# Zero rows under the second chunk product of a delta-rule layer, and a smaller scratch for dynamic DMAs

## The chip, the cores and the metric

The kernel runs on one core of one Trainium2 chip. The core has a matrix engine (TensorE, PE in the profile; its weight loads have a row of their own, PEld), and VectorE (DVE), ScalarE (ACT), GpSimd (POOL) and SyncE (SP), each with its own queue of instructions. The metric is device time in microseconds (us) of one execution, the median of several.

## The reference, cut to what matters

A trunk of two layers on 256 tokens of width 2048. Each layer has a mixing block (one projection whose columns feed RWKV-7 time mixing, dilated attention and a gated MLP, then one output projection) and a feed-forward block. All is float32. The change lies in the time mixing, whose core is the delta rule, 12 heads of 64 channels, one token after the other:

```
def step(state, inp):
    r_t, w_t, k_t, v_t, kk_t, a_t = inp
    sk = jnp.einsum('bhvk,bhk->bhv', state, kk_t)
    state = (state * w_t[:, :, None, :]
             - sk[..., None] * (kk_t * a_t)[:, :, None, :]
             + v_t[..., None] * k_t[:, :, None, :])
    return state, jnp.einsum('bhvk,bhk->bhv', state, r_t)
```

The kernel computes it in two chunks of 128 tokens: within a chunk, all tokens' inner products of two sequences of 64-vectors are formed by matrix products, a triangular matrix is inverted, and the state passes from the first chunk to the second once.

## The kernel before, in words

**The main stream.** Nearly all of TensorE's work is dense products with weights that come from memory in chunks of 512 KB. SP loads a chunk (`raw`), ACT rounds it to the fast format (`whi`, line 104), DVE forms the rest (`wlo`, line 113), and TensorE does three products for each piece of weights: high by high, high by low, low by high (lines 521 to 523 with 256 columns, lines 548 to 550 with up to 512).

**The order.** Python generators emit side work between the pieces of the stream. Each call of `slot()` advances every live generator by one `yield`; it is called about every 12 products of the stream. The order on every engine is thus fixed at build time.

**A pair.** `pair(j)` (line 731) handles heads 2j and 2j+1, one in rows 0 to 63, the other in rows 64 to 127; there are 6 pairs in each layer, 12 in all. For each pair the chunk matrices come from `products(ps)` (line 811), called twice: first for `be` (line 836, tiles `ps_1`), then for `ka` (line 859, tiles `ps_3`). A call goes over 2 heads and 2 chunks. For each it does one product over 128 rows (line 814: high and low parts of a head stacked in the stationary operand `Sp`, the high part of the moving operand twice in `Mv`) and one over the 64 rows of that head (line 815: the same `Sp`, the low part of the moving operand in `Lo`), both into one accumulator. All three lie in one tile, `spl`. A call is 8 products of 256 columns.

**Around a call.** After the first call ACT overwrites the high parts in `Sp` with those of `ka` (line 805), which has to wait until the products that read them are done, and DVE the low parts (line 809). DVE then masks the first results into `A` (line 840), ACT rounds them (`Ah`, line 843), DVE forms `M` (line 848) and `Tm` (line 849), and masks the second halves into `Aqb` (line 851), which frees the accumulators. The second call follows, and right behind it, in the same slot, TensorE transposes `Tm` (line 866, `ps_x`), into an accumulator that line 851 frees. Twelve products of the stream later comes the inversion's first level (line 896).

**The start of a layer.** `start()` (line 627) opens the layer's tiles and lets POOL clear some of them (line 661). In layer 0 POOL then computes the norm of the tokens (line 226) and issues the load of the masks `lvl` (line 398), which DVE waits for (line 184).

Of the kernel before, what the change touches and what calls it, by code (L numbers as in the profile page):

```python
# [20 lines left out]
P = 128  # L21
D = 2048
# [33 lines left out]
def tile_trunk(ctx, tc, x_d, xt_d, pos_d, cst_d, lvl_d, pcol_d, pcv_d, prow_d,  # L56
# [93 lines left out]
    def step(srcs, fn):  # L150
        """weight chunks and the emitter that consumes them"""
        chunks.extend(srcs)
        steps.append(fn)

# [23 lines left out]
    def setup(lvl8):  # L178
        """masks and rotary tables"""
        nc.gpsimd.dma_start(pos_i, pos_d)  # L180
        nc.gpsimd.dma_start(pcols[1], pcol_d[1])
        V.tensor_copy(ident_h, ident)
        yield
        V.tensor_copy(msk, lvl8[:, 6 * P:])
        yield
        V.tensor_copy(lvl.rearrange("p a b -> p (a b)"), lvl8[:, :6 * P])
        ready["tables"] = True
        yield
        pos_f = const.tile([P, 2], F32, name="pos_f")
        V.tensor_copy(pos_f, pos_i)  # L190
        ang = const.tile([P, 16], F32, name="ang")
        for i in range(2):
            V.tensor_scalar(ang[:, i * 8:(i + 1) * 8], cst[:, CS["inv"]:CS["inv"] + 8],
                            pos_f[:, i:i + 1], None, op0=ALU.mult)
        yield
        kr = const.tile([P, 16], F32, name="kr")
        magic = 12582912.0
        for period in (2 * math.pi * 4096, 2 * math.pi):
            V.tensor_scalar(kr, ang, 1.0 / period, magic, op0=ALU.mult, op1=ALU.add)
            V.tensor_scalar(kr, kr, magic, None, op0=ALU.subtract)  # L200
            yield
            rest = period
            for bits in (7, 7, 9, 0):
                if bits:
                    q = 2.0 ** (math.floor(math.log2(rest)) + 1 - bits)
                    c = math.floor(rest / q) * q
                else:
                    c = rest
                rest -= c
                V.scalar_tensor_tensor(ang, kr, -c, ang, op0=ALU.mult, op1=ALU.add)  # L210
            yield
        V.tensor_scalar(ang, ang, math.pi, -math.pi, op0=ALU.min, op1=ALU.max)
        yield
        A.activation(sin, ang, AF.Sin)
        A.activation(cos, ang, AF.Sin, scale=0.5)
        yield
        V.tensor_tensor(cos, cos, cos, op=ALU.mult)
        V.tensor_scalar(cos, cos, -2.0, 1.0, op0=ALU.mult, op1=ALU.add)

# [1 line left out]
    def rsqrt(out, ssq, scale, eps):  # L221
        """out = (ssq*scale + eps)^-0.5"""
        n = ssq.shape[-1]
        t = sm.tile([P, 24], F32, name="rs_t")
        V.tensor_scalar(t[:, :n], ssq, scale, eps, op0=ALU.mult, op1=ALU.add)
        G.tensor_tensor(out, t[:, :n], mhalf[:, :n], op=ALU.pow)

    def sumsq(src, acc, n, junk=None):
        """acc = sum of squares over the n (at most 512) columns of src"""
        if junk is None:  # L230
            junk = pmx.tile([P, 512], F32, name="junk", tag="mx")[:, :n]
        A.activation(junk, src, AF.Square, accum_out=acc)

    def t_block(src, gain):
        """src(i) -> [tok, 128] blocks; returns the split [128 ch, 256 tok] tile times gain"""
        ps = pmx.tile([P, S], F32, name="ps_t", tag="mx")
        for i in range(2):
            T.transpose(ps[:, i * P:(i + 1) * P], src(i), ident)
        ah = const.tile([P, S], F32R, name="act_hi", bufs=KT)
        al = const.tile([P, S], F32R, name="act_lo", bufs=KT)  # L240
        if gain is None:
            A.copy(ah, ps)
            V.tensor_tensor(al, ps, f(ah), op=ALU.subtract)
        else:
            A.activation(ah, ps, AF.Copy, scale=gain)  # L245
            V.scalar_tensor_tensor(al, ps, gain, f(ah), op0=ALU.mult, op1=ALU.subtract)  # L246
        return ah, al
# [7 lines left out]
    def take(n):  # L255
        """count n banks whose readers come later; they must be emitted before the banks go round"""
        while ready["banks"] + n > 4:
            slot()
        ready["banks"] += n
# [14 lines left out]
    def keep_warm(n):  # L274
        """products of zeros while the tensor engine has to wait: its clock falls when it idles"""
        ps = pmx.tile([P, 256], F32, name="ps_w0", tag="mx")
        for _ in range(2 * n):
            T.matmul(ps, warm[:, :P], warm, start=True, stop=True)

    def refresh(yg, yl, rs, c, i, on_dve=True, out=False):  # L280
        """x += yg * rs for one block of 512 columns of a token tile"""
# [10 lines left out]
    class Wave:  # L292
        """the first two column tiles of a product, k tile by k tile"""
# [6 lines left out]
        def part(self, kts, high):  # L300
            """the products with the high or the low parts of these k tiles"""
# [21 lines left out]
    def rows_of(ss, wait=4):  # L323
        """the reciprocal root mean square of the tokens, by partition and as a row on all of them"""
# [24 lines left out]
    def opening(gain0, act, tiles):  # L349
        """the first products, from x as it lies in DRAM by columns"""  # L350
# [59 lines left out]
    def boundary(l, gain0, act, post, tiles):  # L410
        """residual update by columns, the transposed and split input of the next product, and its first two
        column tiles as far as the k tiles have come; the statistics of x come behind"""
# [11 lines left out]
        def tr(g, i):  # L424
            """transposes of k tiles 2g, 2g+1 for one token tile"""
            if i == 0:
                banks[g] = pmm.tile([P, 2, S], F32, name="ps_t", tag="mm")
            for q in range(2):
                kt = 2 * g + q
                T.transpose(banks[g][:, q, i * P:(i + 1) * P], x[:, i, kt * P:(kt + 1) * P], ident)  # L430
# [79 lines left out]
    # products: weights stationary, [128 ch, 256 tok]  # L510
    def ws_step(src, act, out, after):
        """two chunks of 8 k tiles"""
# [20 lines left out]
    # products: activations stationary, 2 x [128 tok, n]  # L533
    def as_steps(src, off, act, k0, nk, n, after, tail=0, more=False, late=0, hold=False):
        """one step per chunk of two k tiles; the last ``tail`` chunks go token tile by token tile"""
# [71 lines left out]
    def mixing(l, post_in):  # L607
# [13 lines left out]
        def rows(t, nm, *ap):  # L621
            """rows of parameters on all partitions"""
# [4 lines left out]
        def start():  # L627
# [11 lines left out]
            # m = 1 + (a - 1) k_a with a = (th + 1) / 2  # L639
# [13 lines left out]
            spl = mp.tile([P, D], F32R, name="spl", tag="rows")  # L653
            env["S"] = spl[:, :4 * P].rearrange("p (h c s) -> p h c s", h=2, c=2)
            env["M"] = spl[:, 4 * P:12 * P].rearrange("p (h c t) -> p h c t", h=2, c=2)
            env["Lo"] = spl[:, 12 * P:].rearrange("p (c t) -> p c t", c=2)
# [7 lines left out]
        def shifted(ps, t, out, done, counted):  # L664
            """token-shifted column tile t of the RWKV projection"""
# [65 lines left out]
        def pair(j):  # L731
# [5 lines left out]
            # decay  # L737
# [7 lines left out]
            # normalised key  # L745
# [5 lines left out]
            # in-context rate  # L751
# [44 lines left out]
            # the operands of the chunk matrices in two parts; one product carries high and low rows of a head  # L796
# [14 lines left out]
            def products(ps):  # L811
                for h in range(2):
                    for c in range(2):
                        T.matmul(ps[h][:, c], Sp[:, h, c], Mv[:, h, c], start=True, stop=False)  # L814
                        T.matmul(ps[h][:, c], Sp[hs[h], h, c], Lo[hs[h], c], start=False, stop=True)  # L815
# [5 lines left out]
            for h in range(2):  # L821
                V.tensor_tensor(Lo[hs[h]], ARf[hs[h]], f(Mv[hs[h], h]), op=ALU.subtract)
# [6 lines left out]
            # chunk matrices, units u = 2*h + c  # L829
# [42 lines left out]
            # T ~ (I + A)^-1 for A as it lies, transposed, by doubling; X = T^T; a level changes the first (X) or  # L872
            # second (T) halves of 2b columns
# [38 lines left out]
            # the last level: one block off the diagonal  # L912
# [14 lines left out]
            # one Newton step with the exact residual  # L927
# [17 lines left out]
            # outputs  # L945
# [43 lines left out]
        def rwkv_post(hf):  # L989
            """group norm, bonus, gate for 6 heads, both chunks"""  # L990
# [228 lines left out]
        def evac_span(a, n):  # L1219
            def after(i, ps):  # L1220
                def g():
# [9 lines left out]
                    elif a == ACOLS:  # L1231
                        if i == 0:
                            zu = tmp("zu", [P, D], 1, tag="rows")
                            env["zu"], env["zrow"] = [zu[:, :GW], zu[:, GW:2 * GW]], zu[:, 2 * GW:]
# [85 lines left out]
        def room(q):  # L1320
            """space of a weight chunk for the next phase, once it is free"""
# [13 lines left out]
    def evac_last(n, yacc, ssq, grow, env, early, out=False):  # L1335
        """sum, its squares, and its product with the gain, for one block of 512 columns"""
# [182 lines left out]
def shape_constants():  # L1519
    """Tables that depend on shapes alone."""  # L1520
# [23 lines left out]
def layout(inp):  # L1544
    """Host side layout of the inputs; nothing but reordering and copies."""
# [24 lines left out]
    def ws(w):  # L1570
        """[L, 2048, n*128] -> [L, n, 128, 16*128]"""
# [3 lines left out]
    def kt_block(w):  # L1575
        """[L, kt*128, n] -> [L, 128, kt*n]"""
# [42 lines left out]
```

## Time and profile before

| | |
|---|---|
| median of 3 runs | 2557.1 us (2555.55 to 2561.63) |
| profiled execution, its own time (span) | 2559.5 us, 2.4 above the median |
| TensorE busy | 2515.6 us (98%), mean granted clock 0.990 |
| TensorE weight loads busy | 2267.8 us (89%) |
| DVE, ACT, POOL busy | 1676.3 (65%), 1266.5 (49%), 596.9 (23%) us |
| mean busy share of the DMA engines | 0.50 |

The busy time of TensorE counts each product from its start to its modelled end, and products overlap, so 98% doesn't say that it works at its peak; how fast it goes is read from the starts of successive products. [...]

### The profile page before, as it was taken

Reading aid. Unit: us, or ns where it says so; the run is one execution under the profiler, and the core shown is the slowest. Engines: PE = TensorE matmul, PEld = TensorE weight load, DVE = VectorE, ACT = ScalarE, POOL = GpSimd, SP = SyncE. Lnnn points to the kernel's source line nnn. Section 1 sums busy time; section 2 is a strip of 40 time slices with the busy share of each in tenths; the row PEclk is TensorE's granted clock in tenths of the full one; section 3 lists DMA queues with packets and bytes.
Section 4 is the critical chain, followed back from the end, with each engine's and each line's share of the span. In section 5 each row is a group of like instructions: output and inputs, shape, how many; then the busy total and the mean of one; then the engine's idle time right before and its main releaser. Section 6 shows DMA issues by size and latency. Waiting matters only on the chain. (4 is left out here: it accounts for less than half of the span.)

```text
span 2559.5 us, 43592 instructions
## 1 busy us (share of the span) xinstructions
PE 2515.6 (98%) x17338; PEld 2267.8 (89%) x17338; DVE 1676.3 (65%) x2376; ACT 1266.5 (49%) x2000; POOL 596.9 (23%) x510
## 2 busy tenths in 40 slices
PE   9999999999999999999999999999999999999998
PEld 8888887899998998998888887878999989989987
DVE  7778866576665565665677787665766655656655
ACT  5444445465554454454464444554655544444443
POOL 4224312032221120120222233131222201202202
PEclk9999999999999999999999999999999999999999
DMA  6343344545555555555543333346555565555554
GB/s 209 125 148 106 109 129 148 193 171 191 183 184 185 190 184 182 194 179 193 196 144 116 116 106 125 113 156 197 174 187 184 180 194 186 181 191 186 181 188 164
DMA packets 119785, 426.73 MB, mean 167 GB/s; under 512 B 13478, under 2 KB 13542, under 8 KB 119070
## 3 DMA queue, kind: packets, MB, share of 16 engines
q1 hardware_dynamic: 115776, 411.09, 48.0%
q0 software_dynamic: 2128, 9.59, 1.1%
q10 hardware_dynamic: 1678, 3.27, 0.5%
q8 instruction: 136, 2.23, 0.3%
q14 instruction: 67, 0.55, 0.1%
HBM read 421.80 MB, written 2.10 MB: 166 GB/s over the span
## 5 line engine op out<-in xcount | busy, mean ns | idle before, releaser
L113 DVE TENSOR_TENSOR wlo<-raw,whi 128x1024 fp32r<-128x1024 f32 (+1 forms) x785 | 972.4, 1246 | 534.5 <-ACT whi L104 533.0
L104 ACT CAST whi<-raw 128x1024 fp32r<-128x1024 f32 (+1 forms) x785 | 808.2, 1033 | 825.3 <-PE ps_up L522 392.8
L521 PE MATMUL ps_up<-act_hi,whi 128*128 128x256 f32 x2752 | 778.9, 283 | 0.0
L522 PE MATMUL ps_up<-act_lo,whi 128*128 128x256 f32 x2752 | 777.4, 282 | 0.0
L523 PE MATMUL ps_up<-act_hi,wlo 128*128 128x256 f32 x2752 | 771.4, 280 | 0.0
L523 PEld LDWEIGHTS ps_up<-act_hi,wlo 128*128 128x128 f32 x2752 | 523.4, 190 | 0.0
L522 PEld LDWEIGHTS ps_up<-act_lo,whi 128*128 128x128 f32 x2752 | 516.6, 188 | 0.2
L521 PEld LDWEIGHTS ps_up<-act_hi,whi 128*128 128x128 f32 x2752 | 514.7, 187 | 0.2
L1438 POOL TENSOR_TENSOR cv<-cv,cv 128x256 f32<-128x256 f32 x88 | 128.9, 1464 | 866.3 <-ACT cv L1436 747.2
L548 PE MATMUL ps_as<-whi,act_hi 128*128 128x512 f32 (+1 forms) x712 | 290.1, 407 | 0.4 <-ACT act_hi L245 0.4
L549 PE MATMUL ps_as<-wlo,hh 128*128 128x512 f32 (+1 forms) x726 | 277.9, 383 | 0.0
L550 PE MATMUL ps_as<-whi,hl 128*128 128x512 f32 (+1 forms) x726 | 277.8, 383 | 0.0
L548 PE MATMUL ps_as<-whi,hh 128*128 128x512 f32 (+1 forms) x726 | 277.8, 383 | 0.0
L550 PE MATMUL ps_as<-whi,act_lo 128*128 128x512 f32 (+1 forms) x712 | 273.9, 385 | 0.0
L549 PE MATMUL ps_as<-wlo,act_hi 128*128 128x512 f32 (+1 forms) x712 | 273.6, 384 | 0.0
L521 PE MATMUL ps_r<-act_hi,whi 128*128 128x256 f32 x576 | 174.9, 304 | 0.0
L523 PE MATMUL ps_r<-act_hi,wlo 128*128 128x256 f32 x576 | 164.6, 286 | 0.0
L522 PE MATMUL ps_r<-act_lo,whi 128*128 128x256 f32 x576 | 164.2, 285 | 0.0
L549 PEld LDWEIGHTS ps_as<-wlo,hh 128*128 128x128 f32 x726 | 136.5, 188 | 26.6
L550 PEld LDWEIGHTS ps_as<-whi,hl 128*128 128x128 f32 x726 | 136.4, 188 | 26.6
L548 PEld LDWEIGHTS ps_as<-whi,hh 128*128 128x128 f32 x726 | 136.4, 188 | 26.5
L550 PEld LDWEIGHTS ps_as<-whi,act_lo 128*128 128x128 f32 x712 | 134.4, 189 | 28.5 <-DVE act_lo L246 0.4
(378 smaller groups left out, 3265.1 us busy)
## 6 DMA issues: line engine op xcount, KB each, us to landing
raw<-in_wup_dram SPq DMA_DIRECT2D x352, 512.0 KB, 4.6
raw<-in_wdn_dram SPq DMA_DIRECT2D x160, 512.0 KB, 3.4
raw<-in_win_t_dram SPq DMA_DIRECT2D x104, 512.0 KB, 3.3
raw<-in_win_r_dram SPq DMA_DIRECT2D x80, 512.0 KB, 3.6
raw<-in_wo_dram SPq DMA_DIRECT2D x64, 512.0 KB, 3.4
raw<-in_wdn_dram SPq DMA_DIRECT2D x32, 256.0 KB, 2.9
xt<-in_xt_dram SPq DMA_DIRECT2D x4, 512.0 KB, 7.2
x<-in_x_dram ACTq DMA_DIRECT2D x4, 512.0 KB, 5.0
```

The costliest lines, as they stand in the source:

```text
L104: A.copy(hi[:, :n], raws[w][:, :n])
L113: V.tensor_tensor(lo[:, :n], raws.pop(w)[:, :n], f(hi[:, :n]), op=ALU.subtract)
L521: T.matmul(ps, hi[:, c], ah, start=kt == 0, stop=False)
L522: T.matmul(ps, hi[:, c], al, start=False, stop=False)
L523: T.matmul(ps, lo[:, c], ah, start=False, stop=kt == 15)
L548: T.matmul(ps, ah[:, t], hi[:, c], start=kt == 0, stop=False)
L549: T.matmul(ps, ah[:, t], lo[:, c], start=False, stop=False)
L550: T.matmul(ps, al[:, t], hi[:, c], start=False, stop=kt == nk - 1)
L1438: G.tensor_tensor(cv[1], cv[0], cv[1], op=ALU.mult)
```

## The change

`Lo` gets a block of columns for each head. Head 0's lower part lies in rows 0 to 63 of its block, head 1's in rows 64 to 127 of its own; the other 64 rows of each block are set to zero once in each layer, by POOL. The second product of `products` then takes all 128 rows of `Sp` and of `Lo`, and the rows that don't belong to the head are multiplied by zeros. The tile `spl` grows from 16 x 128 to 20 x 128 columns, by 2 KB in each partition; the tile `zu`, which takes its place later, grows with it, and its parts stay where they were. [...] Comments and docstrings are gone too; from line 657 on, lines of the changed kernel have numbers one higher.

```
-            spl = mp.tile([P, D], F32R, name="spl", tag="rows")
+            spl = mp.tile([P, 20 * P], F32R, name="spl", tag="rows")
             env["S"] = spl[:, :4 * P].rearrange("p (h c s) -> p h c s", h=2, c=2)
             env["M"] = spl[:, 4 * P:12 * P].rearrange("p (h c t) -> p h c t", h=2, c=2)
-            env["Lo"] = spl[:, 12 * P:].rearrange("p (c t) -> p c t", c=2)
+            env["Lo"] = spl[:, 12 * P:].rearrange("p (h c t) -> p h c t", h=2, c=2)
+            G.memset(f(spl[:, 12 * P:]), 0.0)
...
                         T.matmul(ps[h][:, c], Sp[:, h, c], Mv[:, h, c], start=True, stop=False)
-                        T.matmul(ps[h][:, c], Sp[hs[h], h, c], Lo[hs[h], c], start=False, stop=True)
+                        T.matmul(ps[h][:, c], Sp[:, h, c], Lo[:, h, c], start=False, stop=True)
...
-                V.tensor_tensor(Lo[hs[h]], ARf[hs[h]], f(Mv[hs[h], h]), op=ALU.subtract)
+                V.tensor_tensor(Lo[hs[h], h], ARf[hs[h]], f(Mv[hs[h], h]), op=ALU.subtract)
...
-                            zu = tmp("zu", [P, D], 1, tag="rows")
-                            env["zu"], env["zrow"] = [zu[:, :GW], zu[:, GW:2 * GW]], zu[:, 2 * GW:]
+                            zu = tmp("zu", [P, 20 * P], 1, tag="rows")
+                            env["zu"], env["zrow"] = [zu[:, :GW], zu[:, GW:2 * GW]], zu[:, 2 * GW:4 * GW]
...
-    nc = _bacc.Bacc("TRN2", target_bir_lowering=False, num_devices=1)
+    nc = _bacc.Bacc("TRN2", target_bir_lowering=False, num_devices=1, dynamic_dma_scratch_size=8192)
```

On TensorE, DVE, ACT and SP the same instructions stand in the same order as before. POOL gets one more instruction in each layer. Before, at the start of layer 0, POOL clears the state, the matrix `A` and the three pairs of masked matrices, then computes the norm and loads the masks:

```order
L646 TENSOR_TENSOR rki<-cst,pcol_74 128x12
L661 MEMSET St_363 128x128
L661 MEMSET St_365 128x128
L661 MEMSET A_367 128x512
L661 MEMSET Aqb_369 128x512
L661 MEMSET Aqb_371 128x512
L661 MEMSET Aak_373 128x512
L661 MEMSET Aak_375 128x512
L661 MEMSET Aqk_377 128x512
L661 MEMSET Aqk_379 128x512
L226 TENSOR_TENSOR rstd<-rs_t,mhalf 128x2
L398 DMA lvl_453<-in_lvl_dram 128x1024
```

In the changed kernel the same place reads:

```order
L646 TENSOR_TENSOR rki<-cst,pcol_74 128x12
L657 MEMSET spl 128x1024
L662 MEMSET St_364 128x128
L662 MEMSET St_366 128x128
L662 MEMSET A_368 128x512
L662 MEMSET Aqb_370 128x512
L662 MEMSET Aqb_372 128x512
L662 MEMSET Aak_374 128x512
L662 MEMSET Aak_376 128x512
L662 MEMSET Aqk_378 128x512
L662 MEMSET Aqk_380 128x512
L226 TENSOR_TENSOR rstd<-rs_t,mhalf 128x2
L398 DMA lvl_454<-in_lvl_dram 128x1024
```

The clearing of `spl`, 1024 columns, stands ahead of the others, and the norm and the load of the masks stand behind all of them.

## Rows read from the trace of the kernel before

**Rows 1.** The page's first part: busy us (share of the span), instructions.
```profile
PE 2515.6 (98%) x17338; PEld 2267.8 (89%) x17338; DVE 1676.3 (65%) x2376; ACT 1266.5 (49%) x2000; POOL 596.9 (23%) x510
```

**Rows 2.** TensorE's waits, whole run: who waited for whom, total us, times, longest.
```profile
PE ps_q L896 <- DVE X L907: 3.7, 4, 1.4
PE ps L814 <- DVE spl L809: 2.3, 2, 1.5
PE ps_w L709 <- issue: 1.5, 2, 0.8
```

**Rows 3.** TensorE's groups by line and shape: count, busy us, mean ns, idle before.
```profile
L521 PE MATMUL ps_up<-act_hi,whi 128*128 128x256 f32 x2752 | 778.9, 283 | 0.0
L815 PE MATMUL ps<-spl 64*128 64x256 f32 x96 | 36.9, 384 | 0.0
L814 PE MATMUL ps<-spl 128*128 128x256 f32 x96 | 35.5, 370 | 2.3 <-DVE spl L809 2.3
```

**Rows 4.** Timeline of TensorE, one pair of layer 0: start us, us, instruction.
```profile
256.73 0.36 PE L814 MATMUL ps<-spl 128*128 128x256 f32 x1
...
258.90 0.38 PE L815 MATMUL ps<-spl 64*128 64x256 f32 x1
259.21 0.38 PE L521 MATMUL ps_r<-act_hi,whi 128*128 128x256 f32 x1
259.43 0.28 PE L522 MATMUL ps_r<-act_lo,whi 128*128 128x256 f32 x1
...
260.63 0.28 PE L523 MATMUL ps_r<-act_hi,wlo 128*128 128x256 f32 x1
...
263.24 0.28 PE L814 MATMUL ps<-spl 128*128 128x256 f32 x1
...
265.64 0.40 PE L866 MATMUL ps_x<-ident_h,Tm 128*128 128x128 f16 x4
```

**Rows 5.** Timeline of DVE, the same pair; idle time and its end in brackets.
```profile
257.07 1.23 DVE L113 TENSOR_TENSOR wlo<-raw,whi 128x1024 fp32r<-128x1024 f32 x1
...
259.79 0.42 DVE L809 TENSOR_TENSOR spl<-k,spl 64x256 fp32r<-64x256 f32 x1 [0.75 <-ACT spl L805]
260.23 0.77 DVE L840 COPY_PREDICATED A<-msk,ps 128x256 f32<-128x256 uint8 x2
261.78 0.29 DVE L978 TENSOR_TENSOR sig<-sig,ps_y 128x128 f32<-128x128 f32 x1 [0.78 <-PE ps_y L971]
261.99 1.20 DVE L848 TENSOR_TENSOR M<-Ah,lvl 128x512 f16<-128x512 f16 x1
...
264.41 0.76 DVE L851 COPY_PREDICATED Aqb<-msk,ps 128x256 f32<-128x256 uint8 x2
```

**Rows 6.** Timeline of ACT, the same pair.
```profile
259.36 0.40 ACT L805 CAST spl<-k 64x256 fp32r<-64x256 f32 x1 [0.76 <-PE ps L815]
261.04 0.62 ACT L843 CAST Ah<-A 128x512 f16<-128x512 f32 x1 [1.27 <-DVE A L840]
```

**Rows 7.** Stretches from first to second call: span, busy (x), granted clock, DMA share, GB/s.
```profile
113.10:121.15 8.05, 8.05 (x44) 7.03 (x43) 4.58 (x10) 3.20 (x7) 2.74 (x3) 0.79 0.40 132
256.73:263.24 6.51, 6.51 (x44) 5.48 (x44) 4.57 (x9) 2.92 (x6) 1.51 (x2) 1.00 0.23 81
1338.56:1345.74 7.18, 7.18 (x35) 6.16 (x35) 5.37 (x10) 2.64 (x5) 2.22 (x2) 0.76 0.23 76
```

**Rows 8.** Timeline of POOL at the start of layer 0, last row of layer 1.
```profile
34.20 1.01 POOL L661 MEMSET Aqk<- 128x512 f32 x2
...
36.37 0.79 POOL L398 DMA_DIRECT2D lvl<-in_lvl_dram  x1
...
1328.64 1.08 POOL L761 TENSOR_TENSOR rn<-rn,mhalf 128x4 f32<-128x4 f32 x1 [15.83 <-DVE rn L760]
```

**Rows 9.** Timeline of DVE at the same place.
```profile
42.39 0.29 DVE L184 CAST msk<-lvl 128x256 uint8<-128x256 f32 x1 [3.86 <-DMA lvl<-in_lvl_dram]
```

**Rows 10.** DMA issues by tile and queue: count, KB each, us to landing.
```profile
zu<-in_prow_dram POOLq DMA_DIRECT2D x2, 512.0 KB, 4.4
```

## The prediction

> **What bounds the kernel now.** I read the page first, then TensorE's waits, its groups by line, and the timelines of TensorE, DVE and ACT around the two lines that change. The page says that TensorE is busy for 98% of the span, with weight loads beside it at 89% [rows 1]. The list of its waits agrees: whatever it waits for in and around the pairs is a few microseconds in 2559.5 [rows 2]. So the kernel's time is the sum of what TensorE's products take, one behind the other, and an instruction there is worth its distance to the next start. The groups by line show where that distance is unusual [rows 3]: a product of the stream with 256 columns has a mean of 283 ns, the 64-row one of line 815 with as many columns 384, and line 814, with full 128 rows, still 370. Both means contain overlap, so the timeline decides [rows 4]. In the stream ten starts, from 259.43 to 260.63, take 1.20 us: 0.12 each. In a call of `products` seven starts, from 256.73 to 258.90, take 2.17 us: 0.31 each. The same number of columns goes through, but each change between 128 and 64 rows costs 0.19 us, in both directions. A call thus holds TensorE for 2.48 us (256.73 to 259.21) or, the second one, 2.40 us (263.24 to 265.64). The 24 calls are 58.6 us.
>
> A second loss hangs on the first. From the first call to the second, six of the twelve pairs need 6.43 to 6.51 us at a granted clock of 1.00; four need 8.00 to 8.07 us with the same work at 0.79, and the first pair of each layer needs 7.14 and 7.18 us at 0.76, with no older pair beside it [rows 7]. [...] It costs 8.05 - 6.51 = 1.54 us each time.
>
> **The change part by part.** *Full rows.* If all eight products of a call have 128 rows, no change of rows is left in it, and they should start 0.12 us apart, as in the stream: 8 x 0.12 = 0.96 us for the second call, and I take 1.05 for the first, which comes behind small float32 products. The trace has no product of padded `spl` operands, so bounds: from below the stream's 0.12 [rows 4], from above the 0.31 of today. I take 0.12, because line 814's operands already lie in the same tile with the same type and shape, and only the change of rows sets it apart from line 521. TensorE alone would gain 2.48 - 1.05 = 1.43 and 2.40 - 0.96 = 1.44 us in each pair, 12 x 2.87 = 34.4 us.
>
> *What is late next.* Behind the second call stands the transpose of line 866, which needs `Tm` and an accumulator that line 851 frees. Before, DVE is done with the first half of line 851 at 264.41 + 0.43 = 264.84, TensorE comes at 265.64, and nobody waits [rows 4, 5]. I move both, for this pair. TensorE: first call done at 256.73 + 1.05 = 257.78; the work between the calls is 263.24 - 259.21 = 4.03, so the second call starts at 261.81 and the transpose could start at 262.77. DVE and ACT: the last product of the first call starts at about 257.66 and ends 0.38 later, at 258.04; ACT's second copy of line 805 follows 0.08 behind it as now (258.90 + 0.38, then 259.36 [rows 4, 6]) and ends at about 258.5. DVE is in `wlo` until 258.30 [rows 5] and then does line 809 twice, 0.42 each: done at 259.16 instead of 260.21. Line 840: 259.95. ACT's `Ah`, 0.62: 260.6. Line 978 waits for a product between the calls and moves with TensorE by 1.43, to 260.35 to 260.64. `M` starts at 260.65 instead of 261.99, 1.34 earlier. `Tm` and line 851 keep their distance to it, so the accumulator is free at 264.84 - 1.34 = 263.50, and the transpose starts at about 263.55, 6.82 us behind the first call. TensorE then stands for 0.8 us, and the pair gains 265.64 - 263.55 = 2.09 us, not 2.87.
>
> *The clock.* With 0.12 us between starts a call is as dense as the stream around it, and the stream runs at 1.00. It is a near thing even now: six of the twelve stretches hold a whole call of 2.48 us and stay at 1.00 [rows 7]. So I let the six falls go. The bounds are six kept (0) and six gone (6 x 1.54 = 9.2 us), and the wait before the transpose already takes up a part, since it is DVE's, not the clock's.
>
> *Sum.* Six pairs as above: 6 x 2.09 = 12.5. Four with the fall of the clock: 8.05 + 2.40 - 6.82 = 3.63, times 4 = 14.5. Two first pairs, by the same 6.82: 7.18 + 2.40 - 6.82 = 2.76, times 2 = 5.5. Together 32.5 us.
>
> *The clearing of `spl`.* POOL clears 1024 columns in 1.01 us [rows 8]. In layer 0 it works without a pause through the clearings to the norm and the load of the masks, and DVE stands 3.86 us for those masks [rows 8, 9]; behind it on DVE wait a `wlo` and the low-rank input that TensorE stands for at line 709 [rows 2]. So it goes through to the end: 1.0 us, bounds 0 and 1.0. In layer 1 POOL stands for 15.83 us before its next work on a pair [rows 8], so I take nothing there; if that cover is gone, another 1.0.
>
> *The rest.* `zu` only has more room. [...] I take 0. The waits that change place (line 840 loses its wait for TensorE since line 809 ahead of it already waited; line 870 on POOL gains one for products of the pair before) are over long before, so 0.
>
> Against the profiled execution: 2559.5 - 31.5 = 2528.0. That execution lies 2.4 above the median of the runs, so I forecast 2557.1 - 31.5 = **2525 us** for the median.
>
> **The rivals.** *DVE becomes the bound behind the calls.* DVE is 4.57 us busy of 6.51 between the calls, and no less afterwards, where the levels of the inversion wait for its `X` already now (3.7 us in all [rows 2]). If TensorE catches up with it there, a pair gains no more than DVE's chain does: 1.34 in the six, 1.34 + 1.54 in the four, about 1.05 (the shift of line 809) + 0 in the two: 8.0 + 11.5 + 2.1 = 21.6, less 1.0: 2557.1 - 20.6 = 2536.5. For it: the transpose will wait in each pair. Against: DVE waits for TensorE between the levels too, so there is slack to catch up.
>
> *The change does nothing.* The starts stay 0.31 us apart because what costs is the weight load of each product, not the change of rows. Then the time is 2557.1 + 1.0 = 2558. Against it: in the stream each product has a weight load of its own too and starts at 0.12 [rows 4], and the weight loads are busy 89% beside the products [rows 1]. [...]
>
> *The other side: POOL's queue is blocked by its smaller scratch.* Eight of POOL's loads are issued straight behind another (two behind the masks, two in layer 1's start, and one behind the first in each gated MLP and each feed-forward start). If the scratch holds only one, each has to wait until the one ahead has landed, and the shortest of these landings is 4.4 us [rows 10]: 8 x 4.4 = 35 us, if all lie on the path, against 31.5 gained: 2525 + 35 = 2560, and more with the longer landings. It decides from about 4 us for each of the eight. Against: TensorE hardly ever stands for POOL's loads now, so most would be hidden.
>
> *More than I forecast.* If line 851 is in time after all, the 0.8 us in twelve pairs come back, 2525 - 9.6 = 2515.
>
> **How the numbers follow.** Forecast 0.62, with its own range of 2517 to 2533 (the six falls of the clock, of which one or two may stay or others go, and the waits of 0.8 us by half); DVE as the bound 0.23; more 0.06; nothing 0.05; POOL blocked 0.04. The measurement of this kernel can tell 0.3%, or 7.7 us, from no change; the first three cases all pass that by far. So faster 0.91, the same 0.05, slower 0.04. The range, 2512 to 2542, takes in the forecast, most of the case with DVE and the case of more, and leaves out the last two with some of the edges.
>
> **What would show it.** In the timeline of a pair the eight products of a call should start about 0.12 us apart, and a call take about 1 us; line 814 and line 815 (one higher in the changed kernel) should both come to about 0.28 us in the groups by line. TensorE should stand for `ps_x` behind the second call, for DVE, about 0.8 us in each pair, a wait that the list of before doesn't have. The stretches from first to second call should all be near 5.1 us at a clock of 1.00. The clearing of `spl` should be a row of 1 us at the start of each layer, and line 709 in layer 0 should stand 1.7 instead of 0.7 us. I am wrong in the mechanism if the starts stay at 0.31, and in the size if the wait for `ps_x` is missing, or if new waits for `X` of line 907 or for `wlo` add up to more than 5 us.

## The result, and the profile after

| | median us | lowest to highest | runs | ratio to before, 95% interval |
|---|---|---|---|---|
| before | 2557.16 | 2555.55 to 2561.63 | 4 | |
| changed | 2522.44 | 2519.98 to 2525.13 | 4 | 0.9861 [0.9844, 0.9877] |

The changed kernel is 34.7 us faster by the medians and 36.1 us by the spans of the two profiled executions (2559.5 and 2523.4). The forecast was 2525. The mechanism was right; several terms of the sum were not, and they cancelled.

The page's busy line. TensorE is busy for 43 us less than in [rows 1] and still for 98% of the span, so it is the bound as before:

```profile
PE 2472.7 (98%) x17338; PEld 2248.0 (89%) x17338; DVE 1675.2 (66%) x2376; ACT 1266.5 (50%) x2000; POOL 605.2 (24%) x512
```

TensorE's groups by line and shape (count, total us, mean ns, idle before). Both lines of `products` now stand near the 283 ns of the stream's line 521, where 370 and 384 stood [rows 3]:

```profile
L815 PE MATMUL ps<-spl 128*128 128x256 f32 x96 | 25.2, 294 | 3.2 <-DVE spl L810 2.3 <-ACT bk L857 0.9
L816 PE MATMUL ps<-spl 128*128 128x256 f32 x96 | 24.0, 281 | 0.0
```

TensorE's timeline for the pair that answers to [rows 4]. Seven starts, from 243.67 to 244.38, lie 0.12 apart; the first call holds TensorE for 1.04 us instead of 2.48, the second, from 248.43 to the transpose, for 1.10 instead of 2.40:

```profile
243.46 0.37 PE L815 MATMUL ps<-spl 128*128 128x256 f32 x1
243.67 0.28 PE L816 MATMUL ps<-spl 128*128 128x256 f32 x1
...
244.38 0.28 PE L816 MATMUL ps<-spl 128*128 128x256 f32 x1
244.50 0.28 PE L521 MATMUL ps_r<-act_hi,whi 128*128 128x256 f32 x1
...
248.43 0.28 PE L815 MATMUL ps<-spl 128*128 128x256 f32 x1
...
249.26 0.28 PE L816 MATMUL ps<-spl 128*128 128x256 f32 x1
249.53 0.38 PE L867 MATMUL ps_x<-ident_h,Tm 128*128 128x128 f16 x4
```

The transpose comes 6.07 us behind the first call, not 6.82 as forecast, and with hardly a wait: it starts 0.27 us behind the last product of the call, whose products stand 0.12 apart. DVE and POOL of the same pair say why:

```profile
246.97 0.29 DVE L979 TENSOR_TENSOR sig<-sig,ps_y 128x128 f32<-128x128 f32 x1 [0.27 <-PE ps_y L972]
247.38 0.42 DVE L849 TENSOR_TENSOR M<-Ah,lvl 128x512 f16<-128x512 f16 x1
247.84 1.27 DVE L850 TENSOR_TENSOR Tm<-ident_h,M 128x512 f16<-128x512 f16 x1
249.04 0.76 DVE L852 COPY_PREDICATED Aqb<-msk,ps 128x256 f32<-128x256 uint8 x2
```

```profile
247.43 1.41 POOL L870 TENSOR_TENSOR M<-Ah,lvl 128x512 f16<-128x512 f16 x1 [9.19 <-ACT Ah L844]
```

`M` takes 0.42 us on DVE where it took 1.20 [rows 5]. Both engines wait for ACT's `Ah` and then form a tile of the same form. Before, DVE still had line 978 to do, and POOL started first, at 261.73, DVE's `M` at 261.99 [rows 5]. Now line 979 is over early, DVE starts 0.05 us ahead of POOL, and only the next operation, `Tm`, is slow. The trace of before held both orders: below stand POOL's row of that pair and, from the first pair of layer 1, DVE and POOL with DVE 0.04 us ahead, where `M` took 0.43 us even then:

```profile
261.73 1.17 POOL L869 TENSOR_TENSOR M<-Ah,lvl 128x512 f16<-128x512 f16 x1 [10.21 <-ACT Ah L843]
...
1343.48 0.43 DVE L848 TENSOR_TENSOR M<-Ah,lvl 128x512 f16<-128x512 f16 x1 [0.68 <-ACT Ah L843]
1343.52 1.40 POOL L869 TENSOR_TENSOR M<-Ah,lvl 128x512 f16<-128x512 f16 x1 [8.93 <-ACT Ah L843]
```

The stretches from first to second call (span, busy of PE, PEld, DVE, ACT, POOL with counts, granted clock as a share of full speed, DMA share, GB/s), one for each kind in [rows 7]:

```profile
66.31:70.49 4.18, 4.18 (x35) 4.18 (x35) 3.37 (x7) 1.59 (x4) 0.08 (x1) 1.00 0.32 111
109.94:114.89 4.95, 4.95 (x45) 4.95 (x44) 4.43 (x9) 2.96 (x7) 0.99 (x1) 1.00 0.56 194
243.46:248.43 4.97, 4.97 (x45) 4.97 (x44) 4.45 (x9) 2.79 (x6) 1.00 (x1) 1.00 0.29 106
```

All twelve are at a clock of 1.00; the six falls to a mean of 0.76 to 0.79 are gone. The stretches last 4.9 to 5.0 us, and 4.2 and 4.1 in the first pair of each layer, where 5.1 was forecast for all.

TensorE's waits in the pairs (whom for, total us, times, longest):

```profile
PE ps_q L897 <- DVE X L908: 4.4, 4, 1.4
...
PE ps_dx L905 <- ACT Q L898: 2.3, 4, 1.0
...
PE ps_dx L905 <- DVE Aqk L864: 1.1, 2, 0.6
...
PE ps L815 <- ACT bk L857: 0.9, 2, 0.5
...
PE ps_x L867 <- DVE Aqb L852: 0.2, 1, 0.2
```

The wait for `ps_x`, forecast at 0.8 us in each pair, stands once in this list, with 0.2 us. The starts show more than the list does: over the twelve pairs the transpose stands 0.26 to 0.43 us behind the last product of the call, and 0.12 where nothing holds it (`e4` below), so it is late by 2.3 us in all, against 9.6 forecast. The waits at line 905 are new: the list of before has none for `ps_dx`. Those for DVE's `Aqk` stand in the fourth pair of each layer, beside the group norm, those for ACT's `Q` in the last, beside the rotation of queries and keys. That for `X` was 3.7 us [rows 2]. New too is the wait for ACT's `bk`, 0.5 us inside the second call of the first pair of each layer, and that call lasts 2.0 us.

### The profile page after: what moved, and what is told of

Same layout as the page of the kernel before. It is cut to its first block, busy times and chain, and to the rows that moved or that the text cites. A ratio compares the mean times of both kernels' runs of the same rounds, so it can differ in the third digit from the quotient of the medians.

```text
span 2523.4 us, 43604 instructions
## 1 busy us (share of the span) xinstructions
PE 2472.7 (98%) x17338; PEld 2248.0 (89%) x17338; DVE 1675.2 (66%) x2376; ACT 1266.5 (50%) x2000; POOL 605.2 (24%) x512
```

## The experiments

None of these kernels leaves out a part of the computation. "Before" beside a result is the kernel before on the same chip in the same sitting.

**What a step between 128 and 64 rows costs.** Theory: each change of rows costs 0.19 us. Two kernels on the one before, and a control on the changed one.

*The two 64-row products side by side* (`e1a`):

```diff
-                for h in range(2):
-                    for c in range(2):
+                for c in range(2):
+                    for h in range(2):
                         T.matmul(ps[h][:, c], Sp[:, h, c], Mv[:, h, c], start=True, stop=False)
+                    for h in range(2):
                         T.matmul(ps[h][:, c], Sp[hs[h], h, c], Lo[hs[h], c], start=False, stop=True)
```

> The kernel before, with the products of a call in another order: the two 128-row products of one chunk (head 0, head 1), then the two 64-row ones (head 0 in rows 0-63, head 1 in rows 64-127), then the other chunk. Theory A (a change between 128 and 64 rows costs 0.19 us of start-to-start, both ways): half of the changes are left, starts read 0.12, 0.31, 0.12, 0.31 and so on, a call takes about 1.7 us instead of 2.48. Theory B (what costs is that the weight load of a 64-row product can't overlap a product in the same rows, while other rows run side by side): 128 to 128 at 0.12, the step to the 64-row products and back 0.31 each, and the two 64-row products start almost together (under 0.02 us), as those of the attention's scores do: a call of about 1.5 us. Rival C (a 64-row product is slow by itself): the two 64-row ones stay 0.31 apart, a call of 2.1 us.

One run: 2537.31 us (before 2555.73, 12 runs from 2551.67 to 2561.2). TensorE's timeline, second call and transpose of a pair:

```profile
117.14 0.63 PE L814 MATMUL ps<-spl 128*128 128x256 f32 x2
117.70 0.38 PE L816 MATMUL ps<-spl 64*128 64x256 f32 x2
118.01 0.50 PE L814 MATMUL ps<-spl 128*128 128x256 f32 x2
118.45 0.38 PE L816 MATMUL ps<-spl 64*128 64x256 f32 x2
118.76 0.40 PE L867 MATMUL ps_x<-ident_h,Tm 128*128 128x128 f16 x4
```

The call takes 1.62 us instead of 2.40. The two 64-row products together last 0.38 us, as long as one alone: they lie in different rows, and their starts are 3 to 4 ns apart. The step from the 128-row products to them is 0.31 us in the first chunk and 0.21 in the second, the step back 0.31; and the two 128-row products of a chunk start 0.22 to 0.24 us apart here, not 0.12 as both theories had it. The 3 to 4 ns are those of theory B; the length of the call lies between the two. No clock fall is left in the pairs of this kernel either; over its whole run the granted clock is 0.995, as in the changed kernel.

*Each 64-row product cut in two by columns* (`e1c`, on the kernel before) and *the same cut over full rows* (`e1d`, on the changed kernel). The cut adds a product with the same rows, weights and accumulator, so no change of rows comes in:

```diff
-                        T.matmul(ps[h][:, c], Sp[hs[h], h, c], Lo[hs[h], c], start=False, stop=True)
+                        for q in range(2):
+                            t = slice(q * P, (q + 1) * P)
+                            T.matmul(ps[h][:, c, t], Sp[hs[h], h, c], Lo[hs[h], c, t], start=False, stop=q == 1)
```

> The kernel before, with each 64-row product of a call cut into two of 128 columns, same rows, same weights, one behind the other. No change of rows lies between the two. Theory A (a change of rows costs): the second half starts 0.06 to 0.07 us behind the first, the change to and from stays, and a call takes as long as before, 2.4 to 2.5 us. Theory B (the load of a 64-row product doesn't overlap a product in the same rows): the second half starts 0.25 us (0.31 less the 0.05 of the 128 columns that are missing) behind the first, the next 128-row product as much later, and a call takes about 3.2 us.

> The changed kernel, with each second product of a call (full rows now) cut into two of 128 columns, same weights, one behind the other: the control to the same cut over 64 rows, where the second half started 0.164 us behind the first. If rows are what matters, the halves start 0.06 us apart (128 columns at the 256 columns' 0.12) and a call takes about 1.0 to 1.05 us. If two products of 128 columns with a weight load each are slow in any form, the halves stand 0.11 to 0.16 us apart as over 64 rows, and a call takes 1.2 to 1.5 us.

One run each: 2567.14 us for `e1c` (before 2555.73; its clock is low in eight pairs, 0.989 over the run) and 2532.58 for `e1d` (before 2558.15, 9 runs from 2556.52 to 2562.06). TensorE in a call of each:

```profile
115.24 0.36 PE L814 MATMUL ps<-spl 128*128 128x256 f32 x1
115.53 0.43 PE L817 MATMUL ps<-spl 64*128 64x128 f32 x2
115.89 0.39 PE L814 MATMUL ps<-spl 128*128 128x256 f32 x1
```

```profile
110.47 0.33 PE L818 MATMUL ps<-spl 128*128 128x128 f32 x2
110.64 0.33 PE L815 MATMUL ps<-spl 128*128 128x256 f32 x1
110.81 0.34 PE L818 MATMUL ps<-spl 128*128 128x128 f32 x2
```

Two halves of a 64-row product start 0.164 us apart, two halves of a full-row one 0.060: the same columns, the same weights, no change of rows in either. So the words "each change costs 0.19 us" were too narrow: by them (theory A) 0.164 should have been 0.06 to 0.07, and by theory B 0.25. But these two distances alone are not the price of a product, because the steps beside them change as well. In `e1d` the step into the first half is 0.17 us and the step out of the second 0.11, so the three products take 0.113 each on average, and a call takes 1.39 us instead of 1.03, not the 1.0 to 1.05 that I expected if rows are what matters. In `e1c` a call takes 2.69 and 2.61 us instead of 2.47 and 2.40. Four more products thus cost 0.36 us over full rows and 0.21 over 64: the cut does not show that a 64-row product is slow by its rows alone. The sum of the prediction stood on the distances of whole products, 0.31 and 0.12, and these hold; what the array does in the 0.19 us between them stays open.

**One call at a time.** Both kernels undo the change in one of the calls:

```diff
-            def products(ps):
+            def products(ps, full=True):
...
-                        T.matmul(ps[h][:, c], Sp[:, h, c], Lo[:, h, c], start=False, stop=True)
+                        r = slice(0, P) if full else hs[h]
+                        T.matmul(ps[h][:, c], Sp[r, h, c], Lo[r, h, c], start=False, stop=True)
...
-            products(ps1)
+            products(ps1, False)
```

This is `e3a`; `e3b` has `products(ps3, False)` instead.

> The changed kernel, but the first call of each pair has its second products over 64 rows again; the second call is full. My theory (the chain of ACT and DVE that starts at the end of the first call sets when the transpose behind the second call may start, and the low clock follows the first call): first call 2.48 us, clock down in some pairs again as before, second call 0.96 us, and then TensorE stands for about 0.7 us in front of the transpose in the pairs with an older pair beside them; the gain is nearly gone, about 2548 us. Rival (the two calls are worth the same, 17 us each, and the clock goes by itself): 2540 us, no wait in front of the transpose.

> The changed kernel, but the second call of each pair has its second products over 64 rows again; the first call is full. My theory: first call 1.02 us, second 2.40 us, no wait in front of the transpose, granted clock 1.00 from the first to the second call in all pairs, transpose 7.35 us behind the start of the first call instead of 6.06: 12 x 1.3 = 15 us over the changed kernel, about 2538 us. Rival (the two calls are worth the same and the clock goes by itself): 2540 us with the clock down in about three pairs.

Measured: `e3a` 2546.45 us (2544.74 to 2550.61, 9 runs), ratio 0.9964 [0.9953, 0.9974]; `e3b` 2530.55 (2529.26 to 2532.3, 4 runs), ratio 0.9901 [0.9882, 0.9921].

`e3a` is close to the 2548 us that I expected. DVE starts behind POOL again, `M` takes 1.19 us, and now the wait for `ps_x` is there (rows of POOL, DVE and TensorE in one pair):

```profile
163.13 1.16 POOL L871 TENSOR_TENSOR M<-Ah,lvl 128x512 f16<-128x512 f16 x1 [10.28 <-ACT Ah L845]
163.39 1.19 DVE L850 TENSOR_TENSOR M<-Ah,lvl 128x512 f16<-128x512 f16 x1
...
166.28 0.38 PE L868 MATMUL ps_x<-ident_h,Tm 128*128 128x128 f16 x4 [0.53 <-DVE Aqb L853]
```

The wait that I forecast exists, 4.5 us over nine pairs in the list of this kernel; in eight of the nine `M` is slow. The clock was low in two of its twelve stretches, with an old first call in all twelve:

```profile
112.76:120.80 8.04, 8.04 (x44) 7.02 (x43) 4.57 (x10) 3.20 (x7) 2.74 (x3) 0.79 0.42 132
158.13:164.64 6.51, 6.51 (x44) 5.48 (x44) 4.57 (x9) 2.92 (x6) 1.51 (x2) 1.00 0.26 84
```

In `e3b` the clock is 1.00 in all twelve. In none of the nine traces with a full first call does it fall there. With the old first call it falls in some pairs: six in the trace of before, five in that of `e2` below, which differs from it only in the scratch, two in `e3a` (0.990, 0.992 and 0.993 over the run). In these traces the falls thus come only with an old first call, and it does not decide alone; from one trace each, whether the rows of the second call matter to it can't be told.

`e3b` was better than both theories. Its transposes are as late as I expected in ten pairs (about 7.35 us behind the first call, 1.2 to 1.3 us more than in the changed kernel), but only 0.4 us later in the two first ones: 13.6 us in all, not 15. Yet it loses only 8.1 us by the medians (7.2 by the spans, 10.2 by the ratios). TensorE makes up 5.5 us behind them, by the starts of `ps_dx` and `ps_q` in the fourth and the last pair of each layer. The wait list of `e3b` has nothing for `ps_dx`, and 3.2 us for `X`, where the changed kernel has 3.4 and 4.4. Part of what the second call gains is thus given back later, to DVE, ACT and POOL.

**The scratch alone**, on the kernel before:

```diff
-    nc = _bacc.Bacc("TRN2", target_bir_lowering=False, num_devices=1)
+    nc = _bacc.Bacc("TRN2", target_bir_lowering=False, num_devices=1, dynamic_dma_scratch_size=8192)
```

> The kernel before with nothing but the smaller scratch for dynamic DMAs (8192 bytes). My theory: no effect, within 0.2% of the kernel before, and the loads that POOL issues straight behind one another are issued as close as before (0.55 to 0.8 us). Rival (POOL is blocked until the load ahead has landed): gaps of 4 to 9 us between such issues and a time that is several us longer.

2557.55 us (10 runs; before 2556.11, 13 runs), ratio 1.0004 [0.9994, 1.0015]. POOL's timeline at the start of layer 0 still has three loads straight behind one another:

```profile
36.20 0.79 POOL L398 DMA_DIRECT2D lvl<-in_lvl_dram  x1
36.99 0.55 POOL L180 DMA_DIRECT2D pos_i<-in_pos_dram  x1
37.54 0.54 POOL L181 DMA_DIRECT2D pcol<-in_pcol_dram  x1
```

Nothing is blocked: the rival of the other side falls, and the time belongs to the rows.

**Who starts first, DVE or POOL.** On the changed kernel, one small copy on POOL that reads `Tm`, so that POOL's `M` starts behind both of DVE's operations:

```diff
             yield
+            G.tensor_copy(tmp("gate", [P, 1], 1, F16), Tm[:, 3, P - 1:])
             G.tensor_tensor(M, Ah, bc4(lvl[:, 1]), op=ALU.mult)
```

> The changed kernel, with one tiny POOL instruction ahead of POOL's work on M and Al (lines 870, 871) that reads Tm, so that POOL starts on them only when DVE is done with Tm. My theory (DVE's work on 128x512 16-bit tiles takes 1.2 us instead of 0.42 when POOL is already at work on such a tile, and that made my 1.20 us for M wrong): Tm takes 0.42 us instead of 1.27 in all pairs, line 852 is done 0.85 us earlier, the little wait in front of the transpose goes; time within 2 us of the changed kernel. Rival (Tm is slow by its own operands): Tm stays at 1.27 us and everything behind it is later.

2519.01 us (4 runs), ratio 0.9848 [0.983, 0.9867]; the interval overlaps that of the changed kernel. DVE and POOL in a pair:

```profile
156.12 0.42 DVE L849 TENSOR_TENSOR M<-Ah,lvl 128x512 f16<-128x512 f16 x1
156.58 0.42 DVE L850 TENSOR_TENSOR Tm<-ident_h,M 128x512 f16<-128x512 f16 x1
...
157.07 0.19 POOL L870 COPY gate<-Tm 128x1 f16<-128x1 f16 x1 [10.16 <-DVE Tm L850]
157.21 1.17 POOL L871 TENSOR_TENSOR M<-Ah,lvl 128x512 f16<-128x512 f16 x1
...
158.32 2.16 POOL L872 TENSOR_TENSOR Al<-A,Ah 128x512 f16<-128x512 f32 x1
```

`Tm` falls from 1.27 to 0.42 us, and the transpose comes 5.90 us behind the first call instead of 6.07, 0.12 behind the last product. So the reading of `M` is shown, in both directions (`e1d` has both: in a pair where POOL is 0.11 us ahead `M` is back at 1.35 us, in one where DVE is 0.03 ahead it takes 0.42). What DVE gains POOL loses: `Al` rises from 1.34 to 2.16 us. In the wait list `X` falls from 4.4 to 1.5 us and ACT's `Q`, which waits for POOL, rises from 2.3 to 4.8, while that for `Aqk`, 1.1 us, goes: one wait takes most of the place of the others.

**The changed kernel again, a further padded product, and a shorter queue on POOL.** `e0` is the changed kernel unchanged. `e5` pads the one other 64-row product of a pair, in plain float32; `e6` lets DVE instead of POOL clear the tiles `Q` in the last pair of each layer; `e7` is both:

```diff
+            G.memset(env["a2"][:64], 0.0)
...
-            T.matmul(pa, a2[64:128, jc], wa[64:128], start=True, stop=True)
+            T.matmul(pa, a2[:, jc], wa, start=True, stop=True)
...
-                G.memset(q, 0.0)
+                (V if j == 5 else G).memset(q, 0.0)
```

The first three lines are `e5`, the last two `e6`.

> The changed kernel itself, on the same chip as the next three, to compare them with. All theories: 0.986 of the kernel before, about 2520 to 2522 us, no fall of the clock between the calls of a pair in any of its profiles.

> The changed kernel, with the product of the in-context rate (line 754, 64 rows, two passes in float32, once in each pair) over all 128 rows too: the unused half of its weights is cleared once in each layer by POOL, at a place where POOL has nothing else to do. Now its two passes start 0.32 us apart and the next product 0.31 behind. My theory (64-row products in the same rows don't overlap their loads, full ones do): both at about 0.12 to 0.16 us, 0.35 us less in each pair, 12 x 0.35 = 4 us, about 2518 us. Rival (pairs are bound behind the calls by DVE and POOL now): no gain, within 1 us of the changed kernel.

> The changed kernel, with the clearing of Q (line 877) in the last pair of each layer on DVE instead of POOL. In the changed kernel TensorE stands 0.2 and 0.95 us for Q (line 905 behind ACT's line 898) in the last pair of each layer, while POOL is busy with the rotary embedding. My theory (part of the gain of the full rows is given back because POOL clears Q too late there): these waits go, 2 x 1.1 to 1.5 us less, about 2519 us. Rival (DVE has no room and the wait only moves to DVE's X): no gain.

> The two edits before together. My theory: both gains add up, 4 + 2.5 us less than the changed kernel, about 2515 us. Rival: not below the better one of the two.

| | median us | lowest to highest | ratio, 95% interval |
|---|---|---|---|
| e0 | 2524.58 | 2521.63 to 2530.32 | 0.9873 [0.9853, 0.9893] |
| e5 | 2522.29 | 2519.39 to 2526.18 | 0.9862 [0.9845, 0.9879] |
| e6 | 2520.97 | 2519.09 to 2525.91 | 0.9853 [0.9836, 0.9871] |
| e7 | 2519.97 | 2518.59 to 2523.68 | 0.9854 [0.9838, 0.987] |

All four intervals overlap: none of these edits is told from no change by itself, and the gains that I expected of them (4 us for `e5`, 2 to 3 for `e6`, both for `e7`) don't show in the times. What they did in the trace is plainer. `e5` shortened the two steps behind its product from 0.306 and 0.133 us to 0.216 and 0.029, 0.19 us in a pair and not the 0.35 I expected: in ten pairs its two passes in plain float32 still start 0.32 us apart, at 128 rows as at 64, and only in the first pair of each layer 0.215. In `e6` the long wait of line 905 for ACT's `Q`, 0.95 us in the last pair, is gone; a short one, ahead of it, grew from 0.18 to 0.36 us:

```profile
PE ps_dx L905 <- ACT Q L898: 0.7, 2, 0.4
```

Where the long one came from stands in the timelines of POOL and of ACT in the changed kernel, last pair of layer 0: POOL clears `Q` only behind the rotation of queries and keys, and ACT stands 3.19 us for it.

```profile
304.82 1.58 POOL L1058 TENSOR_TENSOR qkv<-ro,ro 128x192 f32<-128x192 f32 x1
306.34 0.98 POOL L877 MEMSET Q<- 128x512 f16 x2
```

```profile
306.90 0.37 ACT L898 CAST Q<-ps_q 128x256 f16<-128x256 f32 x1 [3.19 <-POOL Q L877]
```

**All three edits together**, `e7` with the small copy of `e4`:

> The changed kernel with the three edits that each did no harm: the in-context rate's product over full rows, the clearing of Q in the last pair on DVE, POOL's work on M and Al behind Tm. If what they save in front of TensorE adds up: 2.3 us (12 x 0.19), 2 to 3 us and about 1 us, so 0.984 of the kernel before, about 2516 us. Rival: the waits only move, 0.986 as the changed kernel.

2513.65 us (2512.51 to 2516.29, 5 runs; before 2558.15, 9 runs), ratio 0.9827 [0.9814, 0.9841]. Its interval ends just below where that of the changed kernel begins, 0.9844, so it beats both kernels, the changed one by a narrow margin. It overlaps those of `e4` and `e7`, so the times don't tell which edit carries it. `e4` shortened the wait for `X` and lengthened that for `Q`; with `e6` in it, that for `X` stays at 1.5 us, that for `Q` is back at 2.4, and that for `Aqk` is gone (waits of this kernel, to be read against the list of the changed one above):

```profile
PE ps_dx L907 <- ACT Q L900: 2.4, 2, 1.2
...
PE ps_q L899 <- DVE X L910: 1.5, 2, 0.8
```

The waits for `X`, `Q` and `Aqk` come to 7.8 us in the changed kernel, 6.3 in `e4`, 6.2 in `e6` and 3.9 here: by the traces they held back a part of the gain, and one edit alone moves most of them to another place.

## Why the prediction was right, and where its terms were off

*Full rows: right.* 0.12 us between starts, calls of 1.04 and 1.10 against 1.05 and 0.96 forecast. The second is longer because 0.27 us, not 0.12, lie between its last product and the transpose: what is left of the wait.

*What is late next: the step that failed.* The prediction put `M` 3.92 us behind the first call, and there it is (247.38 - 243.46). It then let "`Tm` and line 851 keep their distance to it": `M` was counted at 1.20 us because the row of before said so [rows 5], although the two engines' starts, which set those 1.20 us, moved against each other in my own working: ACT's `Ah`, which lets POOL start, came 1.06 us earlier there and DVE's `M` 1.34, more than made up for the 0.26 us that POOL had been ahead. `M` took 0.42, and the 0.78 us between the two are nearly all of the 0.8 us of waiting; 0.14 to 0.31 us were left. From first call to transpose the twelve pairs together went from 114.3 to 72.9 us: a gain of 41.4 us, not 32.5. In the six pairs 8.91 became 6.07 us (2.84 against 2.09 forecast), in the four 10.44 became 6.06 (4.37 against 3.63), and in the two first pairs, which the sum treated like the others, the gain is about 3.4 against 2.76.

*The clock: right.* All six falls went, as taken; in `e3b`, with full rows in the first call alone, the clock is 1.00 in all twelve stretches too. That a call as dense as the stream keeps the clock was an estimate from stretches that stayed at 1.00; what makes it fall, no run shows.

*The clearing of `spl`: too dear.* It takes 0.95 us at 31.56, but the first call of layer 0 starts at 66.31 instead of 66.16: 0.15 us, not 1.0. The norm behind it on POOL (line 226) took 0.74 us instead of 1.25 in the two traces, so the load of the masks went out only 0.35 us later, and DVE took them 0.13 later [rows 9]. One trace can't size so little: the first call starts at 65.70 to 66.49 in the four traces without the clearing and at 65.48 to 67.01 in the ten with it, 0.1 us later on average. The norm took 1.19 to 1.45 us in the four and 0.72 to 0.80 in the ten; why, no run shows.

```profile
31.56 0.95 POOL L657 MEMSET spl<- 128x1024 f32 x1
...
36.03 0.74 POOL L226 TENSOR_TENSOR rstd<-rs_t,mhalf 128x2 f32<-128x2 f32 x1
36.72 0.79 POOL L398 DMA_DIRECT2D lvl<-in_lvl_dram  x1
```

*What was given back: missing.* The rival with DVE as the bound was right in kind, in one pair of each layer rather than in all. By the distances between starts, before against after, 0.72 us go at lines 904/905 in the fourth pair of each layer, where TensorE waits for DVE, and in layer 0 another 0.62 at 896/897 (in layer 1 that wait was 1.4 us long already before). In the last pair of each layer 0.34 and 1.11 go at 904/905, where ACT waits for POOL. Together 5.0 us.

*The sum.* 41.4 - 5.0 - 0.15 = 36.2, beside 36.1 between the two profiled executions. That the forecast of 31.5 came so near is luck: one term was 8.9 too small, another 0.85 too dear, and a third of 5.0 was missing. Of the prediction's own signs for a wrong size the first came, with hardly a wait for `ps_x`. The second came in another place: `X` rose by 0.7 us only, and the new waits are those for `ps_dx`, 3.4 us.

*The rivals.* "Nothing" fell with the starts of 0.12 us: full-row products, each with its weight load, start 0.12 us apart, and filling up the rows of every second product paid. What a product over few rows takes by itself, no run here tests. The sum's 0 for the scratch was an estimate for which no trace of before has a row; `e2`, with the scratch alone, came to 1.0004 [0.9994, 1.0015] of before, and the blocked POOL fell with it. "More" (2515) had the right reason, line 851 in time after all, without what was given back.

## What to carry to other kernels

On the engine that sets the time, read the distance from start to start, not the length of a row, and look for the shape whose distance is out of line with its columns; padding a 64-row operand with zero rows was worth 0.19 us here for nearly every one of the eight products of a call, and 0.19 us for a whole pair in `e5`. Where two engines wait for the same event, ask which of them the change lets start first, because the duration in the old row may belong to that order, as the 1.20 us of `M` did, which became 0.42. A gain at one place can be given back in part where another engine is late, here 5.0 of 41.4 us, so look in each pair apart for what runs beside it.

## What the runs showed of the hardware

- A product of 256 columns over 64 rows, in turn with one over 128 rows, starts 0.31 us behind it [rows 4], the same product over full rows 0.12 (the changed kernel). Two 64-row products in different rows start 3 to 4 ns apart; the steps from full rows to them are 0.21 to 0.31 us, those back 0.31 (`e1a`). Two halves (128 columns) of one 64-row product start 0.164 us apart (`e1c`), of a full-row one 0.060 (`e1d`), though the cut made a call longer by 0.21 us over 64 rows and by 0.36 over full ones.
- In plain float32 filling up the rows of a product of 256 columns left its two passes 0.32 us apart in ten of twelve pairs and shortened the two steps behind it from 0.306 and 0.133 us to 0.216 and 0.029 (`e5`).
- The 128x512 float16 operations `M` and `Tm` of DVE took 0.42 us with POOL not at work (`e4`), `M` 0.42 or 0.43 started 0.03 to 0.05 us ahead of POOL's `M`, and 1.19 to 1.35 where POOL's started 0.11 to 0.26 us ahead. POOL's own `M` took 1.16 or 1.17 us where it started first, 1.40 or 1.41 where DVE did, and its `Al` 1.34 us in the changed kernel and 2.16 in `e4`.
- The smaller scratch for dynamic DMAs changed nothing (`e2`: 1.0004 [0.9994, 1.0015]) with up to three loads issued in a row.
